# A sparse-attention layer's compressed scores with the keys as weights, and its key and value compression on two halves of the array

## The chip, the core and the metric

The kernel runs on one core of a Trainium2 chip. Its time is the device time in microseconds of one execution; the table below gives the runs that were timed. TensorE is the matrix engine, ScalarE and VectorE work on rows of 128 partitions, GpSimd (POOL) does a few clearings and powers, and one queue (SP) issues the loads of weights from memory. Matrix products land in eight accumulator banks of 512 float32 columns.

## What is computed

Two blocks of two layers each, on 256 tokens of width 1024, in float32. The change lies in one layer, the second of the first block: attention with 16 heads of 64 in 4 groups of keys and values, over three branches (compressed, selected, window) whose outputs are added with learned gates. Its compressed branch, cut to what matters:

```python
blocks = t[:, blk_idx] + pe[:, None, :]          # 15 blocks of 32 tokens, stride 16, per group
kc, vc = gelu(blocks_k @ k_w1) @ k_w2, gelu(blocks_v @ v_w1) @ v_w2      # (2048 -> 64 -> 64)
kc = rotary(kc)
s = einsum('bqgrd,bngd->bgrqn', q, kc)           # 256 tokens x 16 heads x 15 blocks
p_cmp = where(vis, softmax(where(vis, s, NEG)), 0)
o_cmp = einsum('bgrqn,bngd->bqgrd', p_cmp, vc)
o = g0 * o_cmp + g1 * o_slc + g2 * o_win
```

With 256 tokens there are 4 blocks to select and 16 may be chosen, so every block is selected: the compressed branch adds to the output, but chooses nothing.

## The kernel before

**Precision.** A product that must be accurate is three matmuls (`mm3`, L419 to L422): operands are split into a high and a low part, and low x high, high x low and high x high add up in one accumulator. A weight piece comes by DMA (`load`, L316) into one of four raw buffers, ScalarE makes its high part (L339), VectorE the low part (L340). Some products (`mm`, L431) are plain float32, which the trace shows as two instructions each.

**Order.** The program is written as generators that are stepped beside each other; a scheduler then orders each engine's queue by the program's order and by when it reckons an instruction to be ready, so that neighbours in a queue can come from different places of the program. The engines take their queues in order.

**The layer** (`nsa`, from L840). After the norm, `t_out` computes the projections of 128 tokens by up to 512 columns, four steps of 12 matmuls: keys of the selected and window branches (L860), keys and values to be compressed (L873), the queries in three groups of 6, 6 and 4 heads (L944 to L960), and the values of the other branches (L1004). Beside the query projections runs the compression (L884 to L937), three steps for each group, first all of the keys, then all of the values: transposes of the tokens (L891), an addition of the position vector on VectorE that puts the 32 tokens of a block on rows (L900, L901), 16 products with the first matrix as weights, 64 columns by 60 streamed (15 blocks of 4 groups; L906), Gelu on ScalarE (L909), and the second matrix. All the 16 products of keys and of values write accumulator partitions 0 to 63. The compressed keys are rotated, transposed and split into `n_kc` (L936); the compressed values go into `vcb` (L919).

**Compressed scores** (`compressed`, L964 to L1000). Beside the last projection, for two halves of the tokens and eight pairs of heads:

```python
o = psum("R")
for t in range(2):
    for p in range(8):
        mm3(o[:, t * S + 32 * p:t * S + 32 * p + 32], sub(qT, A, p, rows128(t)), sub(kc2, A, p // 4), True, True)
```

The 128 x 128 queries of two heads are the weights and 32 columns of keys stream, so that tokens come out on partitions. Mask, maximum, exponential, sum and gate follow on VectorE and ScalarE (L974 to L990), then eight transposes (L997) and two copies (L999) into `pcs`.

**The attention loop** (L1038 to L1072). Sixteen units, eight pairs of heads by two halves of the tokens. `halves3` (L428) computes scores on two row halves of the array, soft-max runs on VectorE and ScalarE (L1029 to L1036), probabilities are transposed (L1055), copied (L1059, L1062) and multiplied with the values (L1066): 64 columns of values as weights, two heads on the two column halves, adding up in a bank half `po`. At the head of each even unit, one product of 256 columns (L1047) starts `po` with the compressed branch. Each unit also steps the second block's context stream once (`hook`), whose matmuls fill TensorE's queue. The output projection (L1073) follows.

Of the kernel before, what the change touches and what calls it, by code (L numbers as in the profile page):

```python
# [232 lines left out]
def _params(i):  # L233

    p = {}
    p["conv_w"] = np.concatenate([_colvec(i["conv_w"][0][k]) for k in range(4)], 1)
    p["conv_b"] = _colvec(i["conv_b"][0])
    p["ga_b"] = _colvec(i["gate_a_b"][0])
    p["gx_b"] = _colvec(i["gate_x_b"][0])
    p["lam"] = _colvec(i["lru_lambda"][0])  # L240
    p["c"] = _colvec(i["c_2"][0])
    p["cc"] = _colvec(i["c_ctx_2"])
    p["b_ada"] = np.concatenate([_colvec(i["b_ada_2"][l]) for l in range(2)], 1)
    p["norm_w"] = np.concatenate([_colvec(i["norm_w_2"][l]) for l in range(2)], 1)
    p["b_mg"] = np.concatenate([_colvec(i["b_merge_2"][l]) for l in range(2)], 1)
    p["an0"] = _colvec(i["attn_norm"][0])
    p["ga_w"] = _bd(i["gate_a_w"][0])
    p["gx_w"] = _bd(i["gate_x_w"][0])
    for n in "kv":
        p["w1_" + n] = i[f"cmp_{n}_w1"][0].reshape(16, 128, 64).transpose(1, 0, 2).reshape(128, 1024)  # L250
    for n in "kv":
        w2 = i[f"cmp_{n}_w2"][0]
        p["w2_" + n] = np.concatenate([w2, np.zeros_like(w2)], 0)
    for n in "kv":
        p["pe_" + n] = i["cmp_pe_" + n][0].reshape(16, 2, 64).transpose(1, 2, 0).reshape(128, 16)
    for l in range(2):
        p[f"fnet{l}"] = _bd(i["w_fnet_2"][l])
        p[f"sp{l}"] = i["w_sp_2"][l].transpose(2, 0, 1).reshape(128, 512)
        p[f"bsp{l}"] = np.repeat(i["b_sp_2"][l].reshape(2, 2, 1, 128), 64, 2).reshape(2, 128, 128).transpose(
            1, 0, 2).reshape(128, 256)  # L260
    return p
# [84 lines left out]
def kernel(ctx: ExitStack, tc: tile.TileContext, x_in, ctx_in, wmain, wctx, wada, params, rows, tabs, out,  # L346
# [493 lines left out]
    def nsa(hook, pre):  # L840
# [34 lines left out]
        for t in range(2):  # L875
            act.activation(cc[:, t, :, 0], heads(o[t]), AF.Copy)
            dve.tensor_copy(cc[:, t, :, 1], heads(o[t]))
        kcb, vcb = buf("n_kc", [2, 2, 32], FR), buf("vc1", [2, 2, 128])
        kc2 = kcb[:, 0], kcb[:, 1]
        with tc.issue_after(marks[2].ins):  # L880
            pool.memset(vcb, 0.0)
        act.activation(kcb.rearrange("p a g n -> p (a g n)"), nsa_m[:, 0:128], AF.Copy)

        def compress(n):  # L884
            blk = buf("fp", [16, 64], FT, 2)
            for g2 in range(2):
                pt = psum("R")
                for j in range(2):
                    for t in range(2):
                        c0 = (0 if n == "k" else 4) + 2 * g2 + j  # L890
                        pe.transpose(pt[:, j * S + t * 128:j * S + t * 128 + 128],  # L891
                                     cc[:, t, c0].rearrange("p b d -> p (b d)"), ident)
                for j in range(2):
                    gi = 2 * g2 + j
                    for b in range(2):
                        r0 = slice(64 * b, 64 * b + 64)
                        w = pt[r0, j * S:(j + 1) * S].rearrange("p (n k b) -> p b k n", k=8, b=2)
                        dst = blk[r0, :, gi * 15:gi * 15 + 15]
                        pb = pe_[n][r0, :].unsqueeze(2)
                        dve.tensor_tensor(dst[:, 0:8], w[:, b, :, 0:15], pb[:, 0:8].to_broadcast([64, 8, 15]), OP.add)  # L900
                        dve.tensor_tensor(dst[:, 8:16], w[:, b, :, 1:16], pb[:, 8:16].to_broadcast([64, 8, 15]),  # L901
                                          OP.add)
                yield
            ph = psum("R")
            for k in range(16):
                mm(ph[:64, :60], w1[n][:, k * 64:(k + 1) * 64], blk[:, k, :60], k == 0, k == 15)  # L906
            hT = buf("n_hT", [4, 32])
            pool.memset(hT, 0.0)
            act.activation(hT[:64, :, 0:15], ph[:64, :60].rearrange("p (g n) -> p g n", g=4), AF.Gelu_apprx_tanh)  # L909
            yield  # L910
            hf = hT.rearrange("p g n -> p (g n)")
            po = psum("R")
            if n == "v":
                for gp in range(2):
                    for b in range(2):
                        mm(po[64 * b:64 * b + 64, gp * 64:gp * 64 + 64], hf[:64, gp * 64:gp * 64 + 64], w2[n][:64, :])
                for b in range(4):
                    r0 = slice(32 * b, 32 * b + 32)
                    dve.tensor_copy(vcb[r0, b // 2, :, 64 * (b % 2):64 * (b % 2) + 64],  # L919
                                    po[r0, :128].rearrange("p (g n) -> p g n", g=2))  # L920
                yield
                return
            mm(po[:, :64], hf[:64, :], w2[n][:64, :])
            z = X.tmp(256)
            kc = z[:, 0:64]
            act.activation(kc, po[:, :64], AF.Copy)
            w = kc[:, 0:16].rearrange("p (h b a c) -> p h b a c", h=1, b=1, a=2)
            s4 = lambda z: z.rearrange("p (h b a c) -> p h b a c", b=1, a=2, c=8)
            rope(w, w, kc_c, kc_s, 1, 1, 8, s4(z[:, 128:144]), s4(z[:, 144:160]))
            dve.tensor_copy(z[:, 64:128], kc)  # L930
            pt = psum("R")
            pe.transpose(pt[:, :128], z[:, :128], ident)
            for half in range(2):
                r0 = slice(64 * half, 64 * half + 64)
                v = pt[r0, :128].rearrange("p (a b n) -> p a b n", a=2, b=2)[:, :, half, 0:16]
                split(v, *sub(kc2, r0, A, slice(16 * half, 16 * half + 16)))  # L936
            yield  # L937

        cmp_ = chain(compress("k"), compress("v"))

        qT = buf("M2", [8, S], FR), buf("M3", [8, S], FR)
        gates = buf("n_gt", [2, 48])
# [20 lines left out]

        def compressed():  # L964

            o = psum("R")
            for t in range(2):
                for p in range(8):
                    mm3(o[:, t * S + 32 * p:t * S + 32 * p + 32], sub(qT, A, p, rows128(t)), sub(kc2, A, p // 4), True, True)
            z, mr = X.tmp(512), X.tmp(64)  # L970
            hn = lambda v: v.rearrange("p (h n) -> p h n", n=16)
            mc, rc = mr[:, :32], mr[:, 32:]
            for t in range(2):
                dve.tensor_tensor(hn(z[:, t * S:(t + 1) * S]), hn(o[:, t * S:(t + 1) * S]),  # L974
                                  cmp_m[:, t * 16:t * 16 + 16].unsqueeze(1).to_broadcast([128, 16, 16]), OP.add)
            yield
            dve.tensor_reduce(mc, hn(z), AX.X, OP.max)
            dve.tensor_tensor(hn(z), hn(z), mc.unsqueeze(2).to_broadcast([128, 32, 16]), OP.subtract)
            act.activation(z, z, AF.Exp)
# [61 lines left out]
        for k, (p, t) in enumerate(units):  # L1041
# [2 lines left out]
                softmax(*units[k + 1], ss[units[k + 1]])  # L1044
            if t == 0:
                po = psum("P")[:, :S]
                mm(po, vcb[:, p % 2, gp], pcs[:, p // 2], True, False)  # L1047

            blocks = ([(0, 0), (1, 0)], [(0, 1), (0, 0), (1, 0), (1, 1)])[t]
            nb = len(blocks)  # L1050
# [12 lines left out]
            for j, (br, kt) in enumerate(blocks):  # L1063
                for h, r0 in enumerate(HALF):
                    c0 = br * 256 + (2 * gp + h) * 64
                    mm(po[r0, rows128(t)], vv[:, kt, c0:c0 + 64], at(pTs, h, j), False, t == 1 and j == nb - 1)  # L1066
            hook(p)
            if t == 1:
                split(po, *sub(oT, A, p))
# [535 lines left out]
```

## Time and profile before

| | |
|---|---|
| runs | 1454.76, 1454.93, 1458.89 us; median 1454.93 |
| profiled execution | 1458.04 us, span 1456.3 us |
| mean granted clock of TensorE | 0.984 of 2.4 GHz |
| TensorE busy with matmuls | 1402.7 us, 96% |
| VectorE, ScalarE, GpSimd busy | 66%, 49%, 3% |
| DMA | 230.31 MB, 158 GB/s |

The span is the time that the profiler saw; the rest of the execution lies around it. "Busy" of an engine counts its instructions; matmuls overlap, so that their durations add up to more than the time they take, and the distance from one start to the next is the better price. A granted clock of 1.00 is 2.4 GHz, 0.50 is 1.2 GHz; a value between them is a window that holds both. In a timeline a row is a start, a length, an engine, a line, what is written and read, and in brackets how long the engine had stood idle and what ended that.

### The profile page before, as it was taken

Reading aid. Unit: us, or ns where it says so; the run is one execution under the profiler, and the core shown is the slowest. Engines: PE = TensorE matmul, PEld = TensorE weight load, DVE = VectorE, ACT = ScalarE, POOL = GpSimd, SP = SyncE. Lnnn points to the kernel's source line nnn. Section 1 sums busy time; section 2 is a strip of 40 time slices with the busy share of each in tenths; the row PEclk is TensorE's granted clock in tenths of the full one; section 3 lists DMA queues with packets and bytes.
Section 4 is the critical chain, followed back from the end, with each engine's and each line's share of the span. In section 5 each row is a group of like instructions: output and inputs, shape, how many; then the busy total and the mean of one; then the engine's idle time right before and its main releaser. Section 6 shows DMA issues by size and latency. Waiting matters only on the chain.

```text
span 1456.3 us, 24385 instructions
## 1 busy us (share of the span) xinstructions
PE 1402.7 (96%) x9815; PEld 1265.0 (87%) x9815; DVE 962.7 (66%) x1675; ACT 710.2 (49%) x1203; POOL 38.6 (3%) x46
## 2 busy tenths in 40 slices
PE   7998999999899999999999999999999999999998
PEld 6887889988697678989888798999999878889997
DVE  7967886645676677768776776354443677665566
ACT  5743446456455664444445575333332345654453
POOL 0010000000000000000000100000000011100000
PEclk9999999999998999999999999999999999999999
DMA  8645777546353026677775553233333516413663
GB/s 295 210 126 189 259 254 234 181 138 196 97 151 117 1 63 211 212 238 231 229 259 178 155 159 89 72 117 103 116 117 116 159 64 184 151 53 109 187 181 124
DMA packets 65745, 230.31 MB, mean 158 GB/s; under 512 B 7776, under 2 KB 9312, under 8 KB 65376
## 3 DMA queue, kind: packets, MB, share of 16 engines
q1 hardware_dynamic: 65632, 228.76, 49.9%
q8 instruction: 77, 1.26, 0.4%
q14 instruction: 36, 0.29, 0.1%
HBM read 227.68 MB, written 1.05 MB: 157 GB/s over the span
## 4 chain that ended last, share of the span: by engine, by line
PE 76%; DVE 9%; DMA 6%; ACT 5%; issue 3%; POOL 1%; SPq 0%; ACTq 0%; DVEq 0%; POOLq 0%
PE P L420 12%; PE P L421 12%; PE P L422 12%; PE Q L420 6%; PE Q L422 6%; PE Q L421 6%; PE R L420 4%; PE R L421 4%; PE R L422 4%; DVE wlo L340 3%; DMA raw<-in_wmain_dram 3%; PE P L431 3%; DMA raw<-in_wada_dram 2%; PE R L428 2%; PE Q L431 2%
## 5 line engine op out<-in xcount | busy, mean ns | idle before, releaser
L340 DVE TENSOR_TENSOR wlo<-raw,whi 128x1024 fp32r<-128x1024 f32 (+2 forms) x325 | 392.1, 1209 | 195.7 <-ACT whi L339 194.1
L339 ACT ACTIVATE whi<-raw 128x1024 fp32r<-128x1024 f32 (+2 forms) x325 | 340.3, 1048 | 323.6 <-PE P L422 80.2
L420 PE MATMUL P<-B,wlo 128*128 128x256 f32 x752 | 216.2, 287 | 0.0
L422 PE MATMUL P<-B,whi 128*128 128x256 f32 x752 | 213.7, 284 | 0.0
L421 PE MATMUL P<-B,whi 128*128 128x256 f32 x752 | 213.4, 284 | 0.0
L420 PE MATMUL Q<-B,wlo 128*128 128x256 f32 x704 | 202.7, 288 | 3.4 <-DVE wlo L340 2.4
L422 PE MATMUL Q<-B,whi 128*128 128x256 f32 x704 | 200.6, 285 | 0.0
L421 PE MATMUL Q<-B,whi 128*128 128x256 f32 x704 | 200.2, 284 | 0.0
L420 PEld LDWEIGHTS P<-B,wlo 128*128 128x128 f32 x752 | 143.8, 191 | 3.0 <-issue 1.4
L421 PEld LDWEIGHTS P<-B,whi 128*128 128x128 f32 x752 | 143.8, 191 | 0.7 <-issue 0.3
L422 PEld LDWEIGHTS P<-B,whi 128*128 128x128 f32 x752 | 143.8, 191 | 0.4 <-issue 0.2
L420 PEld LDWEIGHTS Q<-B,wlo 128*128 128x128 f32 x704 | 135.9, 193 | 7.8 <-DVE wlo L340 4.0
L421 PEld LDWEIGHTS Q<-B,whi 128*128 128x128 f32 x704 | 136.0, 193 | 1.3
L422 PEld LDWEIGHTS Q<-B,whi 128*128 128x128 f32 x704 | 135.9, 193 | 0.3 <-issue 0.2
L420 PE MATMUL P<-whi,B 128*128 128x512 f32 (+3 forms) x264 | 101.4, 387 | 5.3 <-DVE B L411 5.3
L421 PE MATMUL P<-wlo,B 128*128 128x512 f32 (+3 forms) x264 | 99.0, 376 | 0.5 <-DVE wlo L340 0.5
L422 PE MATMUL P<-whi,B 128*128 128x512 f32 (+3 forms) x264 | 98.9, 375 | 0.0
L1091 DVE SCALAR_TENSOR_TENSOR M<-raw,silu_c,M 128x1024 f32<-128x1024 f32 x42 | 53.8, 1281 | 36.9 <-DMA raw<-in_wada_dram 36.8
L420 PE MATMUL R<-C,wlo 128*128 128x256 f32 x272 | 76.3, 280 | 0.0
L421 PE MATMUL R<-C,whi 128*128 128x256 f32 x272 | 76.0, 279 | 0.0
L422 PE MATMUL R<-C,whi 128*128 128x256 f32 x272 | 75.9, 279 | 0.0
L420 PE MATMUL P<-whi,fp 128*128 128x512 f32 x160 | 62.0, 409 | 4.8 <-ACT whi L339 4.8
(485 smaller groups left out, 2856.2 us busy)
## 6 DMA issues: line engine op xcount, KB each, us to landing
raw<-in_wmain_dram SPq DMA_DIRECT2D x324, 512.0 KB, 4.1
raw<-in_wada_dram SPq DMA_DIRECT2D x48, 512.0 KB, 4.4
raw<-in_wctx_dram SPq DMA_DIRECT2D x26, 512.0 KB, 3.9
raw<-in_wmain_dram SPq DMA_DIRECT2D x8, 384.0 KB, 3.1
F<-in_rows_dram SPq DMA_DIRECT2D x4, 512.0 KB, 5.1
C<-in_ctx_dram SPq DMA_DIRECT2D x2, 1024.0 KB, 5.0
C<-in_params_dram SPq DMA_DIRECT2D x3, 512.0 KB, 4.4
ring<-in_rows_dram SPq DMA_DIRECT2D x6, 256.0 KB, 5.3
```

The costliest lines, as they stand in the source:

```text
L339: self.nc.scalar.activation(hi, src, AF.Copy)
L340: self.los.append(self.nc.vector.tensor_sub(lo, src, hi).ins)
L420: pe.matmul(o, l[1], r[0], start=first, stop=False)
L421: pe.matmul(o, l[0], r[1], start=False, stop=False)
L422: pe.matmul(o, l[0], r[0], start=False, stop=last)
L428: pe.matmul(o, l[a], r[b], start=k == 0, stop=k == 2)
L431: pe.matmul(o, l, r, start=first, stop=last)
L1091: dve.scalar_tensor_tensor(a, t, mods[nm][:, k:k + 1], a, OP.mult, OP.add)
```

## The change

Four edits. The first-layer products of keys and of values alternate, keys to accumulator partitions 0 to 63 and values to 64 to 127, with one Gelu over all 128; the second matrix of the values moves to the lower rows to match. The keys' buffer grows to 224 columns a group, zero but for 32 in the middle (and takes the place `C3`, which the first layer's decay table holds before and the loop's exponentials after), so that a slice of 128 columns holds the keys on any of four bands of 32. The scores take such a slice as weights and 256 tokens stream; four pairs of heads add up in half a bank. A copy and four transposes bring the tokens back onto partitions. The compressed branch's value product moves to the end of each unit, with 128 columns.

```diff
-        p["w2_" + n] = np.concatenate([w2, np.zeros_like(w2)], 0)
+        p["w2_" + n] = np.concatenate([w2, np.zeros_like(w2)][::1 if n == "k" else -1], 0)
...
-        kcb, vcb = buf("n_kc", [2, 2, 32], FR), buf("vc1", [2, 2, 128])
+        kcb, vcb = buf("C3", [2, 2, 224], FR), buf("vc1", [2, 2, 128])
...
-        act.activation(kcb.rearrange("p a g n -> p (a g n)"), nsa_m[:, 0:128], AF.Copy)
+        act.activation(kcb.rearrange("p a g n -> p (a g n)").rearrange("p (k n) -> p k n", n=128),
+                       nsa_m[:, None, 0:128].to_broadcast([128, 7, 128]), AF.Copy)
...
-        def compress(n):
-            blk = buf("fp", [16, 64], FT, 2)
-            for g2 in range(2):
...
+        def compress():
+            blks = {}
+            for n in "kv":
+                blk = blks[n] = buf("fp", [16, 64], FT, 2)
+                for g2 in range(2):
...
             ph = psum("R")
             for k in range(16):
-                mm(ph[:64, :60], w1[n][:, k * 64:(k + 1) * 64], blk[:, k, :60], k == 0, k == 15)
+                for n, r0 in zip("kv", HALF):
+                    mm(ph[r0, :60], w1[n][:, k * 64:(k + 1) * 64], blks[n][:, k, :60], k == 0, k == 15)
             hT = buf("n_hT", [4, 32])
             pool.memset(hT, 0.0)
-            act.activation(hT[:64, :, 0:15], ph[:64, :60].rearrange("p (g n) -> p g n", g=4), AF.Gelu_apprx_tanh)
+            act.activation(hT[:, :, 0:15], ph[:, :60].rearrange("p (g n) -> p g n", g=4), AF.Gelu_apprx_tanh)
             yield
...
-            mm(po[:, :64], hf[:64, :], w2[n][:64, :])
+            mm(po[:, :64], hf[k0, :], w2["k"][k0, :])
+            pv = psum("R")
+            for gp in range(2):
+                for b in range(2):
+                    mm(pv[64 * b:64 * b + 64, gp * 64:gp * 64 + 64], hf[v0, gp * 64:gp * 64 + 64], w2["v"][v0, :])
...
-                split(v, *sub(kc2, r0, A, slice(16 * half, 16 * half + 16)))
+                split(v, *sub(kc2, r0, A, slice(96 + 16 * half, 112 + 16 * half)))
...
-        cmp_ = chain(compress("k"), compress("v"))
+        cmp_ = compress()
...
         def compressed():
+            o = psum("R")
+            for gp in range(2):
+                for i in range(4):
+                    c = slice(96 - 32 * i, 224 - 32 * i)
+                    mm3(o[:, gp * S:(gp + 1) * S], sub(kc2, A, gp, c), sub(qT, A, 4 * gp + i), i == 0, i == 3)
+            z = X.tmp(512)
+            act.activation(z, o, AF.Copy)
+            yield
             o = psum("R")
             for t in range(2):
-                for p in range(8):
-                    mm3(o[:, t * S + 32 * p:t * S + 32 * p + 32], sub(qT, A, p, rows128(t)), sub(kc2, A, p // 4), True, True)
+                for gp in range(2):
+                    pe.transpose(o[:, rows128(2 * t + gp)], z[:, gp * S + t * 128:gp * S + t * 128 + 128], ident)
...
             if t == 0:
                 po = psum("P")[:, :S]
-                mm(po, vcb[:, p % 2, gp], pcs[:, p // 2], True, False)
...
-                    mm(po[r0, rows128(t)], vv[:, kt, c0:c0 + 64], at(pTs, h, j), False, t == 1 and j == nb - 1)
+                    mm(po[r0, rows128(t)], vv[:, kt, c0:c0 + 64], at(pTs, h, j), j == 0, False)
+            mm(po[:, rows128(t)], vcb[:, p % 2, gp], pcs[:, p // 2, rows128(t)], False, True)
             hook(p)
```

The compression is stepped as before, three steps for each group of queries; it now has seven where it had eight.

## Rows read from the trace of the kernel before

**Rows 1.** The page: span, and TensorE's busy time, share and instructions.
```profile
span 1456.3 us, 24385 instructions
...
PE 1402.7 (96%) x9815; PEld 1265.0 (87%) x9815; DVE 962.7 (66%) x1675; ACT 710.2 (49%) x1203; POOL 38.6 (3%) x46
```

**Rows 2.** Windows: us, each engine's busy time (instructions), granted clock, DMA share, GB/s.
```profile
409.00:456.90 47.90, 47.90 (x315) 43.40 (x313) 34.16 (x100) 23.51 (x38) 1.10 (x2) 0.89 0.52 152
456.90:527.00 70.10, 65.38 (x473) 47.18 (x472) 51.48 (x231) 49.57 (x173) 0.00 (x0) 0.95 0.06 18
438.00:441.00 3.00, 3.00 (x29) 2.96 (x27) 2.49 (x4) 2.39 (x3) 0.00 (x0) 1.00 0.64 198
442.00:451.00 9.00, 9.00 (x32) 7.94 (x32) 3.36 (x6) 1.06 (x1) 0.00 (x0) 0.50 0.50 150
460.00:464.00 4.00, 3.36 (x21) 2.07 (x20) 3.50 (x19) 3.94 (x18) 0.00 (x0) 1.00 0.50 164
464.50:468.30 3.80, 3.80 (x19) 2.79 (x18) 2.88 (x14) 1.82 (x10) 0.00 (x0) 0.57 0.02 4
...
980.00:1000.00 20.00, 20.00 (x171) 20.00 (x170) 9.98 (x14) 6.12 (x9) 0.00 (x0) 1.00 0.31 96
```

**Rows 3.** Timeline of TensorE: compressed scores, then the last projection.
```profile
438.98 0.26 PE L420 MATMUL R<-n_kc,M 128*128 128x32 f32 x1
...
440.99 0.26 PE L420 MATMUL R<-n_kc,M 128*128 128x32 f32 x1
...
452.01 0.40 PE L420 MATMUL P<-whi,B 128*128 128x512 f32 x1
...
454.08 0.39 PE L420 MATMUL P<-whi,B 128*128 128x512 f32 x1
```

**Rows 4.** Timeline of TensorE (PEld its weight loads) in the attention loop.
```profile
459.76 0.30 PEld L431 LDWEIGHTS P<-F,vc 128*128 128x128 f32 x2 [0.24 <-ACT F L999]
459.76 0.70 PE L431 MATMUL P<-F,vc 128*128 128x256 f32 x2
...
477.09 1.03 PE L1055 MATMUL Q<-ident,C 128*128 128x128 f32 x8
...
480.12 1.09 PE L431 MATMUL P<-ring,fp 128*64 128x128 f32 x14
```

**Rows 5.** Transposes of line 891: shortest/median/longest in ns.
```profile
L891 PE MATMUL R<-ident,M x16: 272/273/299, 411.2 to 428.6; 128*128 128x128 f32 x16
```

**Rows 6.** Timeline of VectorE and ScalarE from the last queries to the first soft-max.
```profile
440.63 0.42 DVE L411 TENSOR_TENSOR M<-Q,M 128x256 fp32r<-128x256 f32 x1
...
448.67 0.68 DVE L978 TENSOR_TENSOR ring<-ring 128x512 f32<-128x512 f32 x1
...
451.50 1.06 ACT L339 ACTIVATE whi<-raw 128x1024 fp32r<-128x1024 f32 x1 [7.58 <-PE P L422]
...
453.87 0.63 ACT L979 ACTIVATE ring<-ring 128x512 f32<-128x512 f32 x1
...
455.64 0.60 ACT L1006 ACTIVATE fp<-P 128x512 f32<-128x512 f32 x1 [0.19 <-PE P L422]
...
457.37 0.69 DVE L990 TENSOR_TENSOR fp<-ring 128x512 f32<-128x512 f32 x1
457.98 0.28 DVE L1029 CUSTOM_DVE_ANT_0 C<-P,T 128x128 f32<-128x128 f32 x1
...
458.82 1.22 DVE L340 TENSOR_TENSOR wlo<-raw,whi 128x1024 fp32r<-128x1024 f32 x1
```

**Rows 7.** Timeline of TensorE: compression, first and second matrix.
```profile
415.98 2.08 PE L431 MATMUL R<-fp,M 128*64 128x60 f32 x32
...
435.26 0.31 PEld L431 LDWEIGHTS R<-n_w,n_hT 64*64 64x64 f32 x8 [0.36 <-ACT n_hT L909]
435.26 0.45 PE L431 MATMUL R<-n_w,n_hT 64*64 64x64 f32 x8
```

**Rows 8.** Groups by line of the stage: busy us, mean ns, idle before.
```profile
L431 PE MATMUL R<-fp,M 128*64 128x60 f32 x64 | 4.4, 224 | 0.0
```

More of the change, by code (lines that the diff above doesn't have):

```diff
@@ L881, in nsa @@
             pool.memset(vcb, 0.0)
-        act.activation(kcb.rearrange("p a g n -> p (a g n)"), nsa_m[:, 0:128], AF.Copy)
-        def compress(n):
-            blk = buf("fp", [16, 64], FT, 2)
-            for g2 in range(2):
[L887 to L903, printed above, removed]
@@ new lines, in nsa @@
+        act.activation(kcb.rearrange("p a g n -> p (a g n)").rearrange("p (k n) -> p k n", n=128),
[5 more added lines that the diff above has]
+                for g2 in range(2):
+                    pt = psum("R")
+                    for j in range(2):
+                        for t in range(2):
+                            c0 = (0 if n == "k" else 4) + 2 * g2 + j
+                            pe.transpose(pt[:, j * S + t * 128:j * S + t * 128 + 128],
+                                         cc[:, t, c0].rearrange("p b d -> p (b d)"), ident)
+                    for j in range(2):
+                        gi = 2 * g2 + j
+                        for b in range(2):
+                            r0 = slice(64 * b, 64 * b + 64)
+                            w = pt[r0, j * S:(j + 1) * S].rearrange("p (n k b) -> p b k n", k=8, b=2)
+                            dst = blk[r0, :, gi * 15:gi * 15 + 15]
+                            pb = pe_[n][r0, :].unsqueeze(2)
+                            dve.tensor_tensor(dst[:, 0:8], w[:, b, :, 0:15], pb[:, 0:8].to_broadcast([64, 8, 15]),
+                                              OP.add)
+                            dve.tensor_tensor(dst[:, 8:16], w[:, b, :, 1:16], pb[:, 8:16].to_broadcast([64, 8, 15]),
+                                              OP.add)
+                    yield
@@ L910, in compress @@
             yield
             hf = hT.rearrange("p g n -> p (g n)")
+            k0, v0 = HALF
             po = psum("R")
[L913 to L922, printed above, removed]
@@ L923, in compress @@
-            mm(po[:, :64], hf[:64, :], w2[n][:64, :])
+            mm(po[:, :64], hf[k0, :], w2["k"][k0, :])
+            pv = psum("R")
+            for gp in range(2):
+                for b in range(2):
+                    mm(pv[64 * b:64 * b + 64, gp * 64:gp * 64 + 64], hf[v0, gp * 64:gp * 64 + 64], w2["v"][v0, :])
             z = X.tmp(256)
@@ L926, in compress @@
             act.activation(kc, po[:, :64], AF.Copy)
+            for b in range(4):
+                r0 = slice(32 * b, 32 * b + 32)
+                dve.tensor_copy(vcb[r0, b // 2, :, 64 * (b % 2):64 * (b % 2) + 64],
+                                pv[r0, :128].rearrange("p (g n) -> p g n", g=2))
             w = kc[:, 0:16].rearrange("p (h b a c) -> p h b a c", h=1, b=1, a=2)
@@ L930, in compress @@
             dve.tensor_copy(z[:, 64:128], kc)
+            yield
             pt = psum("R")
@@ L966, in compressed @@
             o = psum("R")
+            for gp in range(2):
[4 more added lines that the diff above has]
+            act.activation(z, o, AF.Copy)
+            yield
+            o = psum("R")
             for t in range(2):
-                for p in range(8):
-                    mm3(o[:, t * S + 32 * p:t * S + 32 * p + 32], sub(qT, A, p, rows128(t)), sub(kc2, A, p // 4), True, True)
+                for gp in range(2):
+                    pe.transpose(o[:, rows128(2 * t + gp)], z[:, gp * S + t * 128:gp * S + t * 128 + 128], ident)
             z, mr = X.tmp(512), X.tmp(64)
```

## The prediction

> **What bounds the kernel now.** I read the page first: TensorE is busy for 1402.7 of 1456.3 us [rows 1]; no other engine comes near. Work that leaves its queue is a gain, wherever TensorE has no gap. The next view was the windows over the second layer's stage. From 409 to 456.9 us (query projections, compression, compressed scores, last projection) it is busy for all of the 47.90 us, at a mean granted clock of 0.89; in the attention loop after it, for 65.38 of 70.10 us [rows 2]. So the stretch that the change edits is bound by TensorE alone. What the reader is to see is the clock column: 1.00 from 438 to 441, 0.50 from 442 to 451 [rows 2]. For at least 9 us the array ran at 1.2 GHz instead of 2.4, though it never stopped; what it did just before the fall was to stream the compressed scores, 32 columns per load of 128 weight columns. Last, the timeline gave the durations.
>
> **Scores and clock.** Before, there are 16 groups of three matmuls, 48 in all. Eighteen of them take 438.98 to 440.99 at full clock, 112 ns each [rows 3]; the load of the weights must set that, since 32 columns don't fill it. At full clock the 48 are 5.4 us. Behind them stand 36 matmuls of the last projection with 512 columns; nine take 452.01 to 454.08 at full clock, 230 ns each [rows 3], so 8.3 us. Six scores come before 438.98; the other 42 and the 36 would be 42 x 0.112 + 8.3 = 13.0 us. Measured are 17.9, from 438.98 to 456.9. The 4.9 us between are the clock (half of the 9 us at 0.50 is 4.5, the other end).
> After, there are 24 matmuls of 256 columns. In a stretch of nothing else 171 go into 20 us [rows 2], 117 ns each, so 2.8 us. Four transposes come on top at 0.11 (eight take 1.03 us [rows 4], one alone 0.27 [rows 5]), 0.4 us. Scores of 256 columns per load are what that stretch does at clock 1.00, so I take it that the clock stays up. Work: 5.4 - 2.8 - 0.4 = 2.2; clock 4.9; together **7.1 less**. The new copy on ScalarE (512 columns out of an accumulator, 0.60 us [rows 6]) hides behind the 36 projection matmuls; without that cover it costs TensorE its 0.6 and a hand-over. The scores of the last four pairs need the last queries, whose split on VectorE starts at 440.63 before [rows 6]; a wait of up to 1 us there stays in the range.
>
> **Compression.** Before, keys and values each take 32 instructions of 60 columns, all into the lower half of the array. The first 32 take 2.08 us, one alone 0.22 [rows 7, 8], so (2.08 - 0.22)/31 is 60 ns each and all 64 are 3.9 us. After, the same 64 alternate between the two column halves. Nearest is the row of 64 columns into alternating halves: eight in 0.45 us, (0.45 - 0.22)/7 = 33 ns [rows 7]. The other end is the row of alternating halves with 128 columns, fourteen in 1.09 us, (1.09 - 0.27)/13 = 63 ns [rows 4], but with twice the columns; so I take 33: 64 x 33 = 2.1 us, **1.8 less**. Ends: nothing, and 2.3 less at 25 ns, the pace of the loads in the row of eight (0.31 us, one 0.14 [rows 7]). One Gelu in place of two, one clearing less and the later rotation lie on engines that TensorE doesn't wait for in this stretch, so 0; the cover is its own 47.9 us without a gap.
> The halves share all 128 rows, and that speaks against it. The Trainium skill (TensorE: Matmul & The Clock Gate, section The mechanism) says that a weight load overlaps a running matmul only where its row group differs; by that the 1.8 would be 0. The row at 33 ns shows an overlap, but on 64 rows, so no row here settles it.
>
> **The value product.** Eight pairs of 256 columns (0.70 us a pair, less 0.27 of latency [rows 4, 5]) become sixteen pairs of 128 at 2 x 0.11: 3.5 against 3.4 us, **0.1 more**. They move from the head of each even unit to the end of each unit; on TensorE's queue the next scores and transposes stand behind them, and behind those the soft-max on VectorE. The ends are 0 (the loop leaves TensorE 4.7 of 70 us idle) and the price of a pair alone, in rival 4.
>
> **The zero fill.** 896 columns in place of 128 are about 0.9 us of ScalarE, 0.8 more, by the 1.06 of a 1024-column copy [rows 6]. Its new buffer holds the first layer's decay table before, so it can't start until that is read, and stands elsewhere in that queue. It is done long before the stage; I take 0, and 0.8 where a weight conversion for TensorE stands behind it. No transfer is added or moved past another.
>
> **What is late next.** The first unit's soft-max starts on VectorE at 457.98, right behind the last product of the compressed probabilities (457.37) [rows 6]. That chain hung on TensorE itself: its exponential stood behind a weight conversion that had waited 7.58 us for the projection [rows 6], and the same clock shortens that wait. The change puts the copy, four transposes and two hand-overs into the chain: 0.6 + 0.4 + 0.3 (latency) + 2 x 0.2 (a wait of 0.24 for ScalarE [rows 4]) = 1.7 us. Before, 4.5 us lay idle between the subtraction (to 449.35) and the exponential (453.87) [rows 6]; at full clock some 2 of them are left. I book **0.5** of lateness; ends 0 and 2.9 (all 1.7 and one VectorE weight split of 1.22, as stands among the first soft-max now [rows 6], in front).
>
> **Sum:** -7.1 - 1.8 + 0.1 + 0.5 = -8.3 us. The profiled execution took 1458.04 us (the span and 1.7 around it), which makes 1449.7 of it; it lies 3.1 over the median of 1454.93, for which the forecast is **1446.6 us**.
>
> **Rivals.**
> 1. *The clock falls anyway.* It also fell behind a stretch with 3.36 of 4.00 us busy, to 0.57 over 3.8 us [rows 2]; the level isn't safe here, and the short matmuls of the compression stand right in front of the scores. Against it: up to 441 the same compression left it at 1.00. The 4.9 are lost: 1451.5.
> 2. *The halves don't overlap*, and the change doesn't do what its second part says: 64 instructions at 60 ns, 1446.6 + 1.8 = 1448.4. For it stands the 63 ns of the only row with 128 rows and alternating halves; against it, that this row streams twice the columns. The page's rule named above gives this case.
> 3. *The chain to the probabilities is late,* and VectorE, in order, starts the first soft-max behind it: 2.9 in place of 0.5, 1449.0.
> 4. *Slower: TensorE pays at each unit's end.* The value products use all columns and follow products on column halves; a pair alone costs 0.70 us, and TensorE had waited 0.24 before it [rows 4]. Sixteen times 0.94 on the path are 15.0 us, while the eight of before may have lain in the loop's idle time: 1446.6 - 0.1 + 15.0 = 1461.5. It decides from 8.4/16 = 0.53 us per unit. Against it: transposes on all columns stand behind the same products already. The Trainium skill (TensorEngine Tiling (Array Packing), section Key Properties) says that a change of tiling mode drains the array, which leans this way.
>
> **How the numbers follow.** Forecast 0.56, rival 1 0.13, rival 2 0.14, rival 3 0.11, rival 4 0.06. The low end takes compression at 25 ns (0.5), no dip at 464.5 (0.43 x 3.8 = 1.6) and no lateness (0.5): 1446.6 - 2.6 = 1444.0. The high end is rival 1, 1451.5; it takes in rivals 2 and 3 and the wait for the last queries. A measurement of this kernel tells 0.3%, 4.4 us, from no change, so below 1450.6 is faster: the forecast, rival 2 and most of rival 3 make 0.78; rival 1 and the rest make 0.16 for the same; 0.06 slower.
>
> **What would show it.** In the changed kernel's windows: clock 1.00 from the compression to the end of the last projection, and that stretch 7 us shorter; 24 scores near 117 ns; the compression's 64 instructions within 2.3 us; the first soft-max some 8 us earlier, and a loop that still takes near 70 us. The prediction is wrong if the clock shows 0.50 behind the scores, if the compression paces at 60 ns, or if the loop grows by more than 2 us.

## The result and the profile after

The changed kernel is **slower**: 1463.92 us, median of 9 runs (1459.45 to 1474.79), against 1457.54 for the kernel before in 9 runs beside it (1452.49 to 1461.66); ratio 1.0058 [1.0037, 1.0079]. Timed once more, in 12 runs (e11_after_again below), it was 1.0083 [1.0043, 1.0122]. The forecast was 1446.6, faster. The profiled execution of the changed kernel took 1466.41 us. Among the later runs of the kernel before, one of 3421.52 us was slow and stands in no comparison.

The page says little: TensorE's busy time fell by 3.4 us against [rows 1], and the span grew by 8.3.

```profile
span 1464.6 us, 24375 instructions
...
PE 1399.3 (96%) x9811; PEld 1261.1 (86%) x9811; DVE 964.5 (66%) x1675; ACT 710.8 (49%) x1203; POOL 39.4 (3%) x45
```

The windows of the changed kernel answer to [rows 2] (us, each engine's busy time, clock, DMA share, GB/s):

```profile
409.00:453.10 44.10, 43.39 (x313) 38.52 (x311) 35.15 (x96) 23.67 (x39) 0.96 (x1) 1.00 0.59 178
453.10:543.00 89.90, 77.06 (x548) 55.55 (x547) 60.83 (x260) 57.10 (x194) 0.00 (x0) 0.94 0.07 20
...
441.00:451.00 10.00, 9.93 (x59) 8.54 (x58) 8.09 (x12) 5.40 (x7) 0.00 (x0) 1.00 0.69 214
...
460.00:470.00 10.00, 8.70 (x61) 7.07 (x61) 4.88 (x20) 5.26 (x23) 0.00 (x0) 0.83 0.06 23
500.00:510.00 10.00, 8.86 (x53) 6.12 (x51) 7.79 (x36) 5.21 (x20) 0.00 (x0) 0.83 0.01 2
530.00:540.00 10.00, 8.44 (x53) 5.92 (x54) 6.29 (x20) 6.46 (x21) 0.00 (x0) 0.83 0.18 52
```

The first stage did what was forecast: clock 1.00 where [rows 2] had 0.50. The loop did not: TensorE is idle for 12.8 of 89.9 us in it. The clock falls there three times in this profiled execution; but in the kernel before it falls twice, with TensorE idle for 5.5 of the 80 us from 460 to 540:

```profile
460.00:470.00 10.00, 9.17 (x50) 6.59 (x50) 8.54 (x43) 7.73 (x32) 0.00 (x0) 0.83 0.21 67
490.00:500.00 10.00, 8.84 (x50) 6.17 (x49) 8.17 (x40) 8.72 (x28) 0.00 (x0) 0.83 0.00 1
```

To compare stretches I take five marks from the timeline of ScalarE and VectorE: the first key copy of the layer (L863), the first maximum of the soft-max, the last split of `po`, the next layer's norm and, further down, the last layer's norm (both L482). For the changed kernel:

```profile
388.64 0.60 ACT L863 ACTIVATE ring<-P 128x512 f32<-128x512 f32 x1 [1.50 <-PE P L422]
...
454.12 0.28 DVE L1045 CUSTOM_DVE_ANT_0 C<-P,T 128x128 f32<-128x128 f32 x1
...
544.88 0.39 ACT L411 ACTIVATE B<-P 128x256 fp32r<-128x256 f32 x1 [2.90 <-PE P L431]
...
556.38 0.63 ACT L482 ACTIVATE M<-x 128x512 f32<-128x512 f32 x1 [2.42 <-DVE x L614]
...
1185.02 0.63 ACT L482 ACTIVATE M<-x 128x512 f32<-128x512 f32 x1 [10.16 <-PE P L422]
```

and for the kernel before (its second mark is in [rows 6]):

```profile
385.57 0.60 ACT L863 ACTIVATE ring<-P 128x512 f32<-128x512 f32 x1 [1.50 <-PE P L422]
...
539.82 0.39 ACT L411 ACTIVATE B<-P 128x256 fp32r<-128x256 f32 x1 [0.77 <-PE P L431]
...
549.93 0.63 ACT L482 ACTIVATE M<-x 128x512 f32<-128x512 f32 x1 [2.43 <-DVE x L614]
...
1175.56 0.63 ACT L482 ACTIVATE M<-x 128x512 f32<-128x512 f32 x1 [10.16 <-PE P L422]
```

So the 8.3 us are: 3.1 ahead of the layer, **-6.9** to the first soft-max (72.4 to 65.5), **+8.9** in the loop (81.8 to 90.8), +1.4 at the layer's end (10.1 to 11.5), +3.0 in the second block up to the last norm, -1.2 after it. In the first the change touches only the zero fill, in the fifth nothing.

The loop's waits name the place (engine, line, what it waited for: us, times, longest). Of the changed kernel:

```profile
DVE C L1045 <- PE P L428: 15.3, 10, 3.6
ACT ring L1077 <- PE Q L1070: 11.7, 6, 4.7
```

Of the kernel before:

```profile
DVE C L1029 <- PE Q L1055: 8.7, 6, 2.3
```

L428 is the scores, L1055 (now L1070) the transposes of the probabilities. Before, the soft-max stood 8.7 us for the transposes and hardly for its scores; now it waits ten times, 15.3 us, for the scores. TensorE's timeline shows why. Before:

```profile
460.39 0.62 PE L428 MATMUL P<-M,M 64*128 64x256 f32 x3
...
461.75 0.98 PE L428 MATMUL P<-M,M 64*128 64x256 f32 x6
463.29 0.63 PE L1055 MATMUL Q<-ident,C 128*128 128x128 f32 x4 [0.56 <-DVE C L1036]
```

The scores of the unit after next stand ahead of the first unit's transposes (L1055). In the changed kernel they stand behind that unit's value products:

```profile
461.30 0.55 PE L420 MATMUL R<-C,M 128*128 128x256 f32 x1 [2.61 <-DVE kc L411]
...
462.50 1.06 PE L1070 MATMUL Q<-ident,C 128*128 128x128 f32 x4
...
464.96 0.66 PE L431 MATMUL P<-ring,fp 128*64 128x128 f32 x8
465.55 0.49 PE L431 MATMUL P<-F,vc 128*128 128x128 f32 x2
465.97 0.85 PE L428 MATMUL P<-M,M 64*128 64x256 f32 x7
```

That made theory A of the recorded expectations. The scores and `po` take their accumulators from one tag, P, of four banks, handed out in the program's order. The program asks for `po` before it asks for the next scores. Before, `po`'s first writer was the compressed product, whose operands are ready early, so the scheduler could place it, and the scores behind it, far ahead. With the product at the unit's end `po`'s first writer is a value product that needs the soft-max, and the scores can't move ahead of it. Rival B is rival 4 of the forecast: the products at the units' ends cost TensorE their price.

### The profile page after: what moved, and what is told of

Its sections match the earlier page's. It is cut to its first block, busy times and chain, and to the rows that moved or that the text cites. A ratio compares the mean times of both kernels' runs of the same rounds, so it can differ in the third digit from the quotient of the medians.

```text
span 1464.6 us, 24375 instructions
## 1 busy us (share of the span) xinstructions
PE 1399.3 (96%) x9811; PEld 1261.1 (86%) x9811; DVE 964.5 (66%) x1675; ACT 710.8 (49%) x1203; POOL 39.4 (3%) x45
## 4 chain that ended last, share of the span: by engine, by line
PE 75%; DVE 10%; DMA 6%; ACT 5%; issue 3%; POOL 1%; SPq 0%; ACTq 0%; DVEq 0%; POOLq 0%
PE P L420 12%; PE P L421 12%; PE P L422 12%; PE Q L420 6%; PE Q L421 6%; PE Q L422 6%; PE R L420 4%; PE R L421 4%; PE R L422 4%; DMA raw<-in_wmain_dram 3%; PE P L431 3%; DVE wlo L340 3%; DMA raw<-in_wada_dram 2%; ACT whi L339 2%; PE Q L431 2%
```

## The experiments

All 15 in one table; the four whose names begin with r_ are second profiled executions of kernels that stand there already, one run each. The stretches (us) are those between the marks; "lost" is what the clock cost in the loop if its time were all TensorE's: the sum of 1 minus the granted clock over windows of 10 us.

| kernel | median us, runs | ratio to before | L863 at | to soft-max | loop | lost | end | to last norm |
|---|---|---|---|---|---|---|---|---|
| before | (profiled 1458.04) | | 385.6 | 72.4 | 81.8 | 3.4 | 10.1 | 625.6 |
| r_before | one run, 1454.18 | | 387.4 | 70.9 | 80.3 | 1.7 | 10.1 | 623.4 |
| after | 1463.92, 9 | 1.0058 [1.0037, 1.0079] | 388.6 | 65.5 | 90.8 | 5.1 | 11.5 | 628.6 |
| r_after | one run, 1464.00 | | 389.2 | 65.6 | 87.9 | 1.7 | 11.5 | 628.5 |
| e11_after_again | 1466.97, 12 | 1.0083 [1.0043, 1.0122] | 386.5 | 65.5 | 103.5 | 22.2 | 11.5 | 625.7 |
| e1_head | 1451.00, 11 | 0.9964 [0.9952, 0.9976] | 386.4 | 65.5 | 83.2 | 3.4 | 10.1 | 622.5 |
| e10_head_again | 1451.93, 12 | 0.9969 [0.9945, 0.9994] | 388.2 | 65.5 | 83.5 | 3.4 | 10.1 | 624.8 |
| e2_value_only | 1462.07, 7 | 1.0044 [1.0028, 1.0059] | 386.1 | 69.3 | 86.1 | 1.7 | 11.5 | 625.8 |
| e3_scores_first | 1454.97, 12 | 0.9993 [0.9982, 1.0004] | 389.4 | 65.5 | 82.0 | 3.4 | 12.9 | 623.4 |
| r_scores_first | one run, 1459.81 | | 390.1 | 65.4 | 83.2 | 5.1 | 12.9 | 626.9 |
| e4_half_head | 1456.72, 12 | 0.9993 [0.9980, 1.0007] | 392.6 | 65.5 | 81.5 | 1.7 | 11.0 | 624.0 |
| r_half_head | one run, 1453.35 | | 388.2 | 65.5 | 82.7 | 3.4 | 11.1 | 624.7 |
| e5_scores_only | 1451.47, 12 | 0.9971 [0.9957, 0.9985] | 388.6 | 65.7 | 82.4 | 1.7 | 10.1 | 622.7 |
| e6_compress_only | 1456.44, 12 | 1.0001 [0.9983, 1.0019] | 387.6 | 71.6 | 79.5 | 0 | 10.1 | 625.7 |
| e7_head_first | 1454.09, 12 | 0.9984 [0.9971, 0.9998] | 389.3 | 65.5 | 83.9 | 5.1 | 10.1 | 623.0 |
| e8_po_in_R | 1477.32, 6 | 1.0137 [1.0101, 1.0173] | 387.8 | 65.5 | 107.0 | 27 | 10.0 | 625.9 |
| e9_place_only | 1456.87, 12 | 0.9995 [0.9969, 1.0021] | 385.2 | 69.3 | 80.6 | 1.7 | 10.1 | 626.1 |

### The value product put back, moved alone, and its order mended in two ways

**e1_head**, the changed kernel with the product at the head again:

```diff
                 po = psum("P")[:, :S]
+                mm(po, vcb[:, p % 2, gp], pcs[:, p // 2], True, False)
...
-                    mm(po[r0, rows128(t)], vv[:, kt, c0:c0 + 64], at(pTs, h, j), j == 0, False)
-            mm(po[:, rows128(t)], vcb[:, p % 2, gp], pcs[:, p // 2, rows128(t)], False, True)
+                    mm(po[r0, rows128(t)], vv[:, kt, c0:c0 + 64], at(pTs, h, j), False, t == 1 and j == nb - 1)
```

> The changed kernel with the compressed branch's value product put back to the head of each even unit (one product of 256 columns). Measure: the stretch from the first soft-max to the last split of the loop's output, 81.8 us before the change and 90.8 after it. Theory A (claim: the head product was the first to write the pair's accumulator bank, and the scores of the unit after next get their banks only behind that claim; at the end of the unit the claim comes late, and the scores with it): the stretch returns to 80 to 83 us and the scores of unit 2 stand ahead of the transposes of unit 0 again; ratio to the kernel before 0.994 to 0.997. Theory B (price: sixteen products at unit ends cost some 0.4 to 0.9 us each on TensorE's path): the stretch returns as well, 80 to 84; this run alone does not tell A from B. Theory C (the longer chain to the compressed probabilities holds up the first soft-max, and the loop stays late): the stretch stays at 88 or more, ratio 1.003 to 1.007.

**e2_value_only**, the kernel before with the product moved to the units' ends (the same lines the other way round):

> The kernel before with only the value product moved to the end of each unit. Theory A: the stretch from first soft-max to last split grows from 81.8 to 89 to 92 us, ratio 1.005 to 1.009. Theory B: it grows too, by 16 x 0.42 - 8 x 0.35 = 4 us, to 86, ratio 1.002 to 1.004. Theory C: it stays within 1 us of 81.8, ratio 0.999 to 1.001.

**e3_scores_first**, the changed kernel, product at the end, but the next scores asked for ahead of `po`:

```diff
                 softmax(*units[k + 1], ss[units[k + 1]])
+            if k < 14:
+                ss[units[k + 2]] = scores(*units[k + 2])
             if t == 0:
                 po = psum("P")[:, :S]
...
-            if k < 14:
-                ss[units[k + 2]] = scores(*units[k + 2])
             yield
```

> The changed kernel, value product at the end of each unit as it is, but the scores of the unit after next issued ahead of the claim of the pair's bank. Theory A: scores no longer wait for the claim, so the stretch falls to 80 to 84 us and the ratio to 0.994 to 0.998. Theory B: the sixteen products still stand at the unit ends, the stretch stays at 88 to 91, ratio 1.003 to 1.007. Theory C: 88 or more as well.

**e4_half_head**, the first half of the tokens at the head, the second half at the unit's end, 128 columns each, so that `po` has an early writer again:

```diff
                 po = psum("P")[:, :S]
+                mm(po[:, rows128(0)], vcb[:, p % 2, gp], pcs[:, p // 2, rows128(0)], True, False)
...
-                    mm(po[r0, rows128(t)], vv[:, kt, c0:c0 + 64], at(pTs, h, j), j == 0, False)
-            mm(po[:, rows128(t)], vcb[:, p % 2, gp], pcs[:, p // 2, rows128(t)], False, True)
+                    mm(po[r0, rows128(t)], vv[:, kt, c0:c0 + 64], at(pTs, h, j), t == 1 and j == 0, t == 0 and j == nb - 1)
+            if t == 1:
+                mm(po[:, rows128(1)], vcb[:, p % 2, gp], pcs[:, p // 2, rows128(1)], False, True)
```

> The changed kernel with the value product of the even unit at its head (128 columns, which claims the bank early) and that of the odd unit at its end. Still sixteen products, eight of them at unit ends. Theory A: the claim is early, stretch 80 to 84 us, ratio 0.994 to 0.998. Theory B: half of the loss stays, 85 to 87, ratio 0.999 to 1.001. Theory C: 88 or more.

*Measured:* the loop comes back from 90.8 to 83.2 (e1), 82.0 (e3) and 81.5 (e4), and rises from 81.8 to 86.1 where the product alone is moved (e2). e3 has all sixteen products at the units' ends, as the changed kernel has, and e4 eight of them: neither pays B's price in the loop. Taken by itself e2 would not tell A from B: its loop, 86.1, is the 86 that B named and under A's 89 to 92, and its ratio, 1.0044, lies between the two (B up to 1.004, A from 1.005). TensorE's timeline of e4_half_head has the early product and the scores ahead of the transposes again:

```profile
461.65 0.49 PE L431 MATMUL P<-F,vc 128*128 128x128 f32 x2 [0.25 <-ACT F L1015]
462.07 0.61 PE L428 MATMUL P<-M,M 64*128 64x256 f32 x3
...
463.42 0.97 PE L428 MATMUL P<-M,M 64*128 64x256 f32 x6
465.10 0.63 PE L1071 MATMUL Q<-ident,C 128*128 128x128 f32 x4 [0.71 <-DVE C L1052]
```

Its loop waits begin with this line, and the wait for L428 is not among the first:

```profile
DVE C L1045 <- PE Q L1071: 9.9, 6, 3.0
```

In e2_value_only it is the first, as in the changed kernel:

```profile
DVE C L1029 <- PE P L428: 14.4, 10, 3.2
```

*What follows:* by e3 and e4, what the loop loses is the look-ahead of the scores, not TensorE's time for the product. The totals are less tidy: e3 and e4 come out as the kernel before (0.9993, where A had 0.994 to 0.998 and B had 0.999 to 1.001 for e4), 4 to 6 us over e1. Part of it is at the layer's end, where e3 spends 12.9 us and e1 10.1 (the last unit's product and split stand behind everything there); e4 spends 11.0.

### `po` out of the scores' banks

**e8_po_in_R**, the changed kernel but for the tag:

```diff
-                po = psum("P")[:, :S]
+                po = psum("R")[:, :S]
```

> The changed kernel as it is, product at the unit's end, but its accumulator taken from the two banks of the other tag R, so that the four banks of the scores go round without it. Theory A: the scores of the unit after next no longer wait for the value products, their queue places move up, and the loop takes 80 to 86 us in place of 90.8, unless the context stream, which then has one of the two R banks, becomes the wait (to be seen as waits on R). Theory B (each unit's end costs TensorE itself): 88 to 92 us, as in the changed kernel.

*Measured:* 107.0 us for the loop, ratio 1.0137. The scores stand ahead of the first unit's transposes again, though the product is still at the units' ends and the program asks for the scores behind it as before:

```profile
456.44 0.61 PE L428 MATMUL P<-M,M 64*128 64x256 f32 x3
...
460.00 0.63 PE L1070 MATMUL Q<-ident,C 128*128 128x128 f32 x4 [0.56 <-DVE C L1052]
```

The soft-max's wait for the scores is gone from the list, but waits for R, of which the context stream now shares two banks with `po`, are high in it (453 to 540 us):

```profile
DVE C L1045 <- PE Q L1070: 14.7, 9, 4.1
ACT B L411 <- PE R L431: 13.3, 5, 3.2
DVE C L1237 <- PE R L431: 8.4, 2, 4.5
ACT cq L411 <- PE R L1165: 6.5, 2, 3.4
```

And the clock is low, 27 us lost in the loop:

```profile
470.00:490.00 20.00, 20.00 (x96) 15.17 (x97) 9.92 (x42) 7.61 (x29) 0.00 (x0) 0.50 0.00 1
```

*What follows:* with nothing but the tag changed, the scores' place and the missing wait show that it was the claim of a bank of P that held the scores back. By its time the run decides nothing: the loop missed A's 80 to 86 by 21 us, and the waits on R that its expectation had named and the low clock are not told apart here.

### Each part by itself, and both mends together

**e5_scores_only**: the kernel before with the diff's lines for the key buffer, its fill, the split's slice and `compressed`, and no others. **e6_compress_only**: the kernel before with the diff's lines for `compress` and for the second matrix of the values, and no others. **e7_head_first**: e1's lines and e3's lines together.

> The kernel before with the second part of the change alone: keys as weights, 256 tokens streaming, the wider key buffer and its zero fill, the copy and the four transposes; compression and value product as before. The forecast's steps give -7.1 for work and clock, +0.5 for lateness: some 6.6 us less than before (ratio 0.9955), the clock at 1.00 behind the scores, and from the first query split (L863) to the first soft-max some 66 us where before had 72.4. Rival, compression does more than booked: the stretch falls by only 4 to 5 us here. Rival, the longer chain spoils the start of the loop: the loop (84 us or more from first soft-max to last split, before 81.8) gives back over 2 us.

> The kernel before with the side-by-side compression alone. If a weight load on one column half overlaps the matmul on the other, 64 instructions pace at 30 to 33 ns and the stretch is 1.8 us shorter: ratio near 0.9988, not to be told from no change by the total, but from L863 to the first soft-max 70 to 71 us where before had 72.4, with the clock still at 0.50 behind the 32-column scores. If it hides nothing (the stretch is not bound by this work) the stretch stays at 72.4.

> The changed kernel with the compressed value product back at the head of the even unit and, besides, the scores of the unit after next written ahead of it. Theory A (a bank is handed out in the program's order, and the product at the unit's end kept the scores behind it): nothing is left to free, the loop takes 81 to 83 us. If the 4 us by which the two mended kernels (scores first; half a product at the head) lie over the one with the product at the head come from the order of the loads in front of the next layer, which this kernel has like the latter, the total is near 1451 (ratio 0.996 to 0.997). If they come from the earlier place of the scores, it is near 1455 (0.999).

*Measured:* the scores alone give 4.7 us (0.9971), nearly all that e1, with both parts, has. Its loop, 82.4, stays under the 84 of the rival with the longer chain. The compression alone gives nothing by the total (1.0001), and 71.6 us to the first soft-max, above the 70 to 71 that were expected, lies between two executions of the kernel before (72.4 and 70.9), though its pace is as forecast. In the changed kernel, TensorE:

```profile
427.16 2.08 PE L431 MATMUL R<-fp,M 128*64 128x60 f32 x62
```

(2.08 - 0.22)/61 = 30.5 ns an instruction, against 60 in [rows 7]. But from L863 to the first compressed score (at 440.87 in the changed kernel, below) it is 52.2 to 52.3 us in all twelve traces with the compression side by side, and 52.6 to 52.7 in the five without: 0.4 us, not 1.8. The weight loads of the changed kernel's projection say where some of the rest went:

```profile
421.31 0.19 PEld L420 LDWEIGHTS P<-whi,B 128*128 128x128 f32 x1 [0.25 <-ACT whi L339]
422.80 0.19 PEld L421 LDWEIGHTS P<-wlo,B 128*128 128x128 f32 x1 [0.72 <-DVE wlo L340]
```

These waits stand ahead of the side-by-side products. Before, the keys' products, 2.08 us from 415.98 [rows 7], stood in front of this part of the projection; now they come behind it, at 427.16, so TensorE reaches these weights earlier, and ScalarE and VectorE, which convert them, do not. Two such waits, 1.0 us of loads, stand where before had none. Matmuls leave TensorE idle for 0.64 us from 412 to 441, where before it had no gap; what took the remainder is not shown.

e7 has a loop of 83.9, no better than e1's, as A said, though above the 81 to 83 it had named (the clock took 5.1 of it), and a total between the two outcomes of its expectation, so it doesn't say what the 4 us are.

### What lies outside the layer

Four second profiled executions of unchanged kernels; **e9_place_only** (`buf("n_kc", [2, 2, 32], FR)` becomes `buf("C3", [2, 2, 32], FR)` in the kernel before); and two kernels timed again on one chip.

> The kernel before, unchanged, a second profiled execution. If the stretches that the change doesn't touch differ by chance from execution to execution, the start of the attention layer (L863, 385.6 in the first) and the time from the next layer's norm to the last layer's norm (625.6) move by 1 to 3 us, while from L863 to the first soft-max (72.4) and the loop (81.8) repeat within 1 us. If they belong to the kernel, all four repeat within 0.5 us.

> The changed kernel, unchanged, a second profiled execution. Chance: L863 (388.6) and the later stretch (628.6) move by 1 to 3 us, the stretch to the first soft-max (65.5) and the loop (90.8) repeat within 1 us. Belonging to the kernel: all repeat within 0.5 us.

> The kernel with half of the value product at the head, a second profiled execution. Its first began the layer latest of all (L863 at 392.6), with the same instructions before it. Chance: near 386 to 390 now. Belonging to the kernel: 392 to 393 again. The loop (81.5) within 1 us in either case.

> The kernel with the scores written ahead, a second profiled execution. Chance: L863 (389.4) and the later stretch (623.4) move by 1 to 3 us. Belonging to the kernel: they repeat within 0.5 us. The loop (82.0) and the way from its last split to the next norm (12.9, where the kernel before had 10.1) repeat within 1 us in either case.

> The kernel before with nothing changed but the place of the key buffer: C3 in place of its own, still 128 columns; its fill then waits for the decay table's last read and stands two weight conversions later in ScalarE's queue. If the place costs the stretches ahead of the attention layer something, L863 begins at 388 to 390 (looks so far: 386 to 388 with the old place in four, 386 to 393 with C3 in ten) and the total is 2 to 3 us over the kernel before (ratio 1.002). If it costs nothing, the ratio is 1.000 within its interval and L863 lies at 386 to 388.

> The changed kernel with the value product back at the head, as in the first of the experiments, timed again beside the changed kernel on one chip. By the layer's own stretches (158.8 us from L863 to the next norm, against 167.7 and 165.0 in two looks at the changed kernel) it is 6 to 9 us ahead of the changed kernel; by the earlier medians, each against its own runs of before, 13.7. If only the layer differs, 6 to 9; if the value product's place reaches beyond the layer, 12 to 15.

> The changed kernel as it is, timed again beside the one with the product at the head. If only the layer differs from the kernel before (162.8 us there and 166.4 here, means of two looks each), the ratio to the kernel before is 1.002 to 1.003; if the loss of the first timing repeats, 1.0055.

*Measured:* L863 moves by 0.6 to 4.4 us between two executions of one kernel, the second block's stretch by 0.1 to 3.5; the place of the key buffer costs nothing that can be measured (0.9995). The loop repeats less well than the 1 us that was expected: it moves by 1.2 to 2.8 us in the four pairs. To the first soft-max the kernels with the new scores take 65.4 to 65.7 us in all traces; the kernel before does not repeat (72.4, 70.9, and 69.3 in e9), and its low clock lasts 9 us in the first trace and less in the others.

The layer begins later on the mean where the zero fill is wide: L863 at 386.4 to 392.6 us in the twelve traces that have it (mean 388.7), at 385.2 to 387.6 in the five with the narrow fill (mean 386.4). e9 has the new place but the narrow fill, so the width was not tried by itself. The stretch in which the fill stands, between the norms (L482) at some 65 and 117 us, takes 52.2 us on the mean in both groups; the difference shows between the norms at 127 and 366, where the change touches nothing, so its cause is open.

What was not expected is the loop of e11_after_again: 103.5 us. Its windows:

```profile
487.00:493.00 6.00, 3.96 (x39) 2.74 (x36) 3.93 (x18) 5.14 (x20) 0.00 (x0) 1.00 0.02 4
499.00:505.00 6.00, 4.86 (x35) 3.46 (x31) 5.61 (x24) 3.46 (x14) 0.00 (x0) 0.85 0.00 0
505.00:541.00 36.00, 35.25 (x154) 23.82 (x152) 17.35 (x81) 16.09 (x59) 0.00 (x0) 0.50 0.00 1
541.00:547.00 6.00, 4.96 (x30) 3.33 (x31) 3.06 (x14) 3.00 (x8) 0.00 (x0) 0.74 0.00 0
547.00:553.00 6.00, 5.49 (x36) 4.15 (x36) 3.72 (x7) 3.44 (x11) 0.00 (x0) 1.00 0.29 87
```

TensorE, idle for a third of 487 to 493 and again for 1.1 us of 499 to 505, falls to 1.2 GHz at about 503, and stays there for some 40 us. The runs' mean clocks tell how often: of the 21 timed runs of the changed kernel 7 have a clock of 0.958 to 0.977 and take 1470.97 to 1478.53 us; 3 have 0.983 to 0.984 and take 1466.8 to 1467.3; 11 have 0.987 or more, median 1462.43. In the 95 runs of the kernels that have the look-ahead (e1, e3 to e7, e9, e10) the lowest is 0.982. The kernel before had one such run too (0.913, 1470.66) in 85, and the next lowest is 0.981. e2, which waits for its scores in the same way, has 0.985 or more in all its 7 runs, too few to tell.

*What follows:* with "lost" taken off, the loop is 78 to 81 us in all traces with the look-ahead and 84 to 86 in e2 and the first two of the changed kernel (81 in e11, where "lost" seems to count too much: waits need not stretch as the matmuls do). So the wait itself costs about 6 us and the layer's end 1.4. The clock adds nothing certain in the calmer traces, 1.7 to 5.1 us lost, as the kernels with the look-ahead lose 0 to 5.1; in e11 it takes some 20 more. e10 and e11 are 15.0 us apart in their medians, more than the 6 to 9 of the layer's first traces. In the two profiled executions they are 20.8 us apart, and the layer alone, 159.2 against 180.4 us, holds all of it. Among runs at a good clock (0.987 or more) e11 has a median of 1460.64 (5 runs), 8.7 us over e10: inside the 6 to 9.

*Open:* over both timings the changed kernel's runs at a good clock are 11 us over e1 and e10 (1451.36, 23 runs), of which its two calmer traces show 6 to 9 in the layer; the rest shows in the second block (628.6 and 628.5 in those traces, 625.7 in the third, 622.5 and 624.8 in e1 and e10), where the difference by chance is nearly as large. e4's total, 5.7 us over e1 with the same layer, is open in the same way. That the idle time brings the clock down was not tried by itself; it rests on the order of events in these traces and on the count of runs.

## Why the prediction was wrong

**The failed step is the value product.** The text said "0.1 more", from the work of 16 pairs against 8, took the value near "0" for the move, and put its doubts in rival 4, a price on TensorE. It named what stands behind the product on TensorE's queue, but asked only how long the product takes. What the move changed is who writes `po` first: an instruction that is ready early was replaced by one that waits for the soft-max, and as accumulators of a tag are handed out in order, all scores behind it lost their head start. In place of 0.1 it cost about 6 us in the loop and 1.4 at its end, and a third of the changed kernel's runs have a low clock besides; e2, the move alone, is 6.2 us slower than the kernel before (1.0044). Rival 4 gave nearly the right total, 1461.5, for a wrong reason: in the changed kernel the pair of products takes 0.42 us from its start to the next (465.55 to 465.97 above; 0.25 to 0.45 at all sixteen), not 0.94, and e3 pays it sixteen times with a loop like that of before.

The text had said what would show it wrong, a loop that grows by more than 2 us; it grew by 8.9.

**Scores and clock: right in kind, a little large.** TensorE's timeline of the changed kernel, against [rows 3]:

```profile
440.87 0.28 PE L420 MATMUL R<-M,C 128*128 128x256 f32 x1
...
442.05 0.28 PE L421 MATMUL R<-M,C 128*128 128x256 f32 x1
...
447.03 0.60 PE L985 MATMUL R<-ident,ring 128*128 128x128 f32 x4
...
452.72 0.39 PE L422 MATMUL P<-whi,B 128*128 128x512 f32 x1
```

The first score and the last projection product of the kernel before:

```profile
438.20 0.18 PE L420 MATMUL R<-n_kc,M 128*128 128x32 f32 x1
...
456.58 0.39 PE L422 MATMUL P<-whi,B 128*128 128x512 f32 x1
```

Eleven scores start from 440.87 to 442.05, 118 ns each where 117 were forecast; the clock stays at 1.00, so rival 1 is out in this stage. From the first score to the start of the last projection product it was 18.4 us and is 11.9: 6.5 less, where 7.1 were booked. But the 4.9 of clock belonged to one execution: the same way takes 16.7 us in r_before and 15.1 in e9. So the median gained less than the profiled execution could, 4.7 us in e5 where 6.6 were expected.

**Compression: pace right, worth wrong.** 33 ns were taken and 30.5 measured, so the halves overlap and rival 2 is out. The Trainium skill (TensorE: Matmul & The Clock Gate, section The mechanism), by which a load overlaps only where the row group differs, is contradicted by these 62 instructions: all use 128 rows. The step that failed is "the cover is its own 47.9 us without a gap": a stretch without gaps was taken as one that stays without them. With the keys' products no longer in front, TensorE caught up with two weight conversions, and 0.4 of 1.8 us was left.

**Zero fill: right where it stands.** ScalarE, changed kernel:

```profile
86.69 0.95 ACT L883 ACTIVATE C<-T 128x896 fp32r<-128x896 f32 x1 [1.78 <-DVE ring L781]
```

ScalarE had stood idle for 1.78 us before it, and e9 finds no price for its place. The later start of the layer in the traces with the wide fill is told above and stays open.

**Lateness: 0.5 booked, about 1.6 found, in another place.** The first maximum comes 1.4 us after the start of the last projection product, as before; but VectorE now takes the unit's four maxima among the steps of the chain, and its next work behind the fourth starts at 456.53, 2.4 us after the first maximum; in [rows 6] that is 0.84 (457.98 to 458.82). VectorE is so about 1.6 us later at the loop's head, in e1 and e5 too (2.4 there as well); that the loop gives back as much of the 6.9 was not tried. Rival 3 had that order of size.

Without the value product the forecast's direction holds: e1, the change but for that edit, is 0.9964 and 0.9969 of the kernel before, e5 0.9971. Either beats both kernels, by 3.6 to 4.9 us against the kernel before, where 8.3 were forecast for the whole.

## What to carry to other kernels

Before moving an instruction, ask whether it is the first writer of a buffer that is handed out in turn: its readiness then sets how far everything that asks later can be placed ahead, whatever its own time. A gain on an engine that is busy all through a stretch is worth only what its suppliers can follow; ask how far ahead of it they are, not for its gaps alone. And a stall in a TensorE loop may cost twice, the wait and then the clock, so compare the clock of several executions.

## What the runs showed of the hardware

- Matmuls of 64 weight columns and 60 streamed, on all 128 rows, run at 30.5 ns each when they alternate between the column halves (62 in 2.08 us) and at 60 ns on one half (32 in 2.08 us, [rows 7]).
- The granted clock fell in two kinds of place: behind 32 columns streamed per load without a pause of the array (0.50 for 9 us in [rows 2]), and in a loop where TensorE waits (0.83 over 10 us several times, in the kernel before too; 0.50 for 20 us in e8 and for 36 us in e11). In the second kind how long it stayed low differs from execution to execution. The Trainium skill (TensorE: Matmul & The Clock Gate, section A second HAM failure mode: psum-queue depth-cycling) tells of a kernel that cycles through accumulator banks, whose small pauses made the clock go up and down; the loops here agree in kind, the changed kernel's with 1.7 to 5.1 us lost and e11's fall as its worst case.
